# A hybrid layer on one core: a new written order for the recurrence's blocks, a low-rank product on full rows, and two more blocks that read PSUM

## The chip, the cores and the metric

The kernel runs on one core of a Trainium2 chip. The metric is the device time of one execution in microseconds (us); the median of three runs is given. A core has TensorE (PE, which multiplies and writes to the accumulator memory PSUM; PEld is its weight load), VectorE (DVE), ScalarE (ACT), GpSimd (POOL) and SyncE (SP), whose queue issues most of the transfers here. All of them share the on-chip memory SBUF. Each engine works through its own list of instructions in order, and waits for the others by semaphores.

## What is computed

One decoder layer on 2048 tokens of width 1024. Two mixers read the same normalised input, their outputs are joined by `w_out`, and a gated feed-forward part follows. All of it is float32 in the reference:

```python
xn = _rms_norm(h, pre_mix_norm[l])
proj = (xn @ w_in[l]).astype(jnp.float32)
p_ssd, p_rwkv = jnp.split(proj, [SSD_COLS], axis=-1)
y_ssd = _ssd_mixer(p_ssd, ...)        # causal conv of 4 taps, chunked scan, gate, norm
y_rwkv = _rwkv7_mixer(p_rwkv, ...)
mix = jnp.concatenate([y_ssd, y_rwkv], axis=-1).astype(h.dtype) @ w_out[l]
h = h + _rms_norm(mix, post_mix_norm[l])
```

The part that the change touches is the second mixer (8 heads of 64), together with the projections and the causal convolution of the first:

```python
p = p + (_token_shift(p) - p) * mu                       # this token mixed with the one before
r, w_lo, k, v, a_lo, g_lo = jnp.split(p, ...)
w_log = -softplus(-(w0 + tanh(w_lo) @ w2)) - 0.5         # two low-rank products, 64 rows each
a = sigmoid(a0 + a_lo @ a2)
kk = heads(k * k_k); kk = kk / max(norm(kk), 1e-12)
# per token: S = S * decay + (S @ -kk) (kk * a)^T + v k^T ;  y = S @ r
```

## The kernel before

`phase_R` computes the recurrence and the shared projections, `phase_S` the first mixer's scan and the output projection, and the feed-forward part comes last. The change touches `phase_R`, which works on 16 blocks of 128 tokens. In iteration `it` the block `it` is the front (`f`): its input is projected. The block before it (`b`) is finished behind it, the block two back (`a`) gets its last norm and store, and the next one (`n`) is loaded.

A block's work is cut into named steps (the methods of `Block`), and a step into numbered parts. For a front these are:

- `d.g` (14 of them) and `c`, written `conv.g` (8): float16 products of the block with a weight tile, 24 matmuls each at L324. Two neighbours share one PSUM bank of tag `mm`, which has two buffers. From `d`, ScalarE takes this token's part and VectorE adds the previous token's (`past`, L535). From `c`, ScalarE begins the sum of four taps in `ca` (L571) and VectorE adds six taps for the pair (L581); then come a tanh (L587) and a product (L592).
- `low.i`: the two low-rank products into `zw` and `za`. Weights and values are split into a high and a low half in float16. Four matmuls at L622 use all 128 rows, four at L626 the 64 rows of `wl`'s third plane.
- `scan`, `keys`, `norm`: running sums of the decay into `Pv`, their exponentials `Pi` and `Pv`, the keys' norm (product `nq` at L667, Ln L678, Exp L679, `kkn` L680), the scaled keys `tk` (L683), and the matrices `AR` (L684, L700) and `BK` (L688, L690).
- `gram.c`, for the two halves `c` of a block: products `gr` of `AR` with `BK` (L713), masked into `G` (L718).
- `solve`: the small triangular systems. `G`'s corners go to DRAM and back into `atl`; then 31 pairs of a product (L753) and a sum (L759) on VectorE run through them, and the result goes over DRAM (`XTd`, L765) back into `XT` (L771), in four transfers.

For the back block follow `turn` (transposes `XW`, L824), `merge` (products `pw` L840 and `po` L844), `own.c` (`pq`: the local products L873 and those with the state L879), `update.c` (`pu`, L897), `state.c` (`pS` L921, the new state `S` L927, the reads L932 into `pq`), `gate` (`zg`) and `finish` (norm, the transposes `yt`, the output `yo` and its store `YR`, L1000).

The order is written out by hand. `FIRST` holds for iteration 0, `SECOND` for 1, `PLAN` for 2 to 14, `LAST` for 15 and `DRAIN` for 16. An entry `f.norm/2` is part 2 of the front's step `norm`; where VectorE, ScalarE, GpSimd and SP run under `manual_schedule`, each engine gets its instructions in the order of the table. `PLAN` is one period of a loop that is wound around: the parts of a block's solve from some step on stand at the start of the table, for the block before. At iterations 2 and 15 the loop `if it in (2, iters - 1)` first emits those parts that the period before or after would have held.

A block whose `direct` is true lets ScalarE and VectorE read `d` and `c` from PSUM. Otherwise a copy is made first (`raw` in `d`, `rc` in `conv`), GpSimd begins the taps, and `scan` gets one more Ln of a single column (L651). Before, `direct` was true for the blocks 2 to 14.

Of the kernel before, what the change touches and what calls it, by code (L numbers as in the profile page):

```python
# [18 lines left out]
P = 128  # L19
# [198 lines left out]
PLAN = """  # L218
b.solve/30 b.solve/31 b.d.13/1 b.solve/32 b.solve/33 f.d.0 f.d.1/0 f.d.1/1 a.finish.0/1 b.conv.5/10 b.solve/34
a.gate/1 b.solve/35 b.d.13/3 b.d.13/4 n.load/1 b.solve/36 f.d.2 b.solve/37 b.solve/38 f.d.1/2 f.scan/2 a.finish.0/2  # L220
b.solve/39 a.state.1/3 a.finish.0/3 a.finish.0/4 f.d.1/3 b.values/0 b.solve/40 a.finish.1/0 b.solve/41 b.solve/42
b.solve/43 b.solve/44 b.solve/45 f.low.0/0 b.values/1 f.low.0/1 f.low.0/2 b.solve/46 b.solve/47 b.solve/48
a.finish.1/1 b.solve/49 b.solve/50 b.solve/51 b.values/3 b.values/4 f.d.1/4 b.transposed.1/1 a.finish.1/2 b.solve/52
a.finish.1/3 a.finish.1/4 b.conv.5/11 f.d.3/0 f.low.1/0 f.low.1/1 f.low.1/2 a.finish.1/5 b.values/2 b.own.0/0 f.d.3/1
f.d.3/3 b.solve/53 f.low.0/3 f.d.4 b.solve/54 b.solve/55 f.d.3/2 f.low.0/4 f.d.5/0 b.conv.7/9 a.finish.1/6 f.d.3/4
b.solve/56 b.conv.7/10 f.d.5/2 f.low.1/5 f.d.5/4 f.d.5/1 f.low.1/9 f.d.6 f.d.5/3 f.keys/0 b.solve/57 b.solve/58
f.d.7/0 a.finish.1/7 f.low.1/6 f.keys/1 f.low.1/3 b.solve/59 f.low.1/7 f.d.8 f.d.7/2 b.solve/60 b.solve/61 b.solve/62
b.solve/63 f.low.1/8 b.solve/64 f.norm/0 f.low.1/4 b.solve/65 f.d.7/1 b.solve/66 b.solve/67 f.norm/1 f.d.7/4 f.scan/0
a.state.1/4 f.norm/2 b.solve/68 b.solve/69 b.solve/70 f.d.7/3 b.own.0/1 b.solve/71 f.scan/1 a.finish.1/8 f.norm/4
f.norm/5 f.norm/7 b.solve/73 f.norm/6 b.solve/74 b.state.0/0 f.d.9/0 f.d.9/2 f.norm/3 f.scan/3 f.d.9/4 f.d.9/1 f.d.9/3  # L230
n.load/0 b.solve/72 f.norm/9 f.conv.0 b.solve/75 f.scan/4 f.norm/10 b.solve/76 f.conv.1/0 f.conv.1/1 f.conv.1/2
f.conv.2 f.conv.1/3 f.conv.1/5 f.conv.1/4 f.conv.1/6 b.conv.7/11 f.conv.3/0 f.conv.1/8 b.solve/78 f.conv.1/7
f.conv.3/1 f.conv.3/2 b.turn/0 f.norm/8 b.turn/1 f.conv.4 b.own.0/2 f.conv.1/9 f.load/10 b.merge.0/0 f.conv.3/3
f.conv.3/4 f.receptance/0 f.norm/11 a.finish.1/9 b.merge.0/2 f.conv.3/6 f.conv.5/0 f.norm/12 b.solve/77 b.merge.0/1
b.merge.1/0 f.gram.0/0 n.load/2 n.load/3 b.merge.1/2 b.merge.1/1 f.conv.1/10 b.update.0/0 f.conv.3/8 f.gram.1/0
f.conv.1/11 f.conv.3/5 f.conv.3/7 f.gram.0/1 f.conv.3/9 f.conv.3/10 f.gram.0/2 f.solve/8 b.update.0/1 n.load/4
f.solve/1 f.gram.1/2 f.gram.1/1 b.state.0/5 f.conv.5/1 f.conv.5/2 b.state.0/2 f.solve/0 n.load/5 f.conv.6 f.conv.5/3
n.load/6 f.transposed.0/0 b.state.0/3 f.conv.3/11 f.solve/2 f.conv.5/4 f.receptance/3 f.conv.5/5 b.state.0/1
f.conv.5/6 f.conv.7/0 b.state.0/6 b.own.1/0 b.state.0/4 f.receptance/2 f.conv.7/1 b.low.0/6 f.conv.7/3 f.solve/3
f.solve/4 f.solve/6 f.solve/5 f.conv.7/2 f.conv.7/4 f.receptance/1 f.conv.5/8 f.conv.7/5 b.state.1/0 f.conv.7/6  # L240
b.own.1/1 f.transposed.0/1 f.conv.7/8 b.state.1/1 f.solve/7 n.load/8 f.conv.5/7 f.transposed.1/0 f.conv.7/7 f.solve/9
b.gate/0 f.solve/10 b.own.1/2 b.update.1/0 f.d.10 f.conv.5/9 f.solve/11 n.load/7 f.d.11/0 f.receptance/4 f.solve/12
f.solve/13 f.solve/14 f.d.12 f.solve/15 f.solve/16 f.solve/17 f.solve/18 f.solve/19 f.solve/20 f.solve/21 f.solve/22
f.solve/23 f.solve/24 f.d.11/1 f.solve/25 f.solve/26 b.update.1/1 b.state.1/2 b.state.1/5 f.d.13/0 f.low.0/5 f.d.11/2
f.transposed.0/2 f.solve/27 f.d.11/4 b.state.1/6 b.finish.0/0 n.load/9 f.solve/28 f.solve/29 f.d.11/3 f.d.13/2
"""
# [82 lines left out]
def phase_R(tc, K, const, tables, x, w_r, w_c, wl_d, g2_d, XN, XC, YR, filler, iters=16):  # L329
    nc = tc.nc  # L330
    V, S, G_ = nc.vector, nc.scalar, nc.gpsimd
    with ExitStack() as ctx:
# [85 lines left out]
        class Block:  # L418


            def __init__(self, it):
                self.it, self.sf, self.direct = it, f"_{it}", 1 < it < iters - 1
                self.todo, self.m = {}, {}
# [86 lines left out]
            def d(self, g):  # L510
# [86 lines left out]
            def low(self, part):  # L597
# [19 lines left out]
                def products(i):  # L617
                    own, X = sides[i][0], self.X
                    ps = m["z", i] = self.ms(("zw", "za")[i])
# [4 lines left out]
                    for j in range(4):  # L624
                        js = slice(j * P, (j + 1) * P)
                        nc.tensor.matmul(  # L626
                            ps[:, j, :], wl[own, 2, js], X[own, i], start=False, stop=j == 3, skip_group_check=True)

# [389 lines left out]
        for it in range(iters + 1):  # L1018
# [10 lines left out]
            if it in (2, iters - 1):  # L1029
                for step in PLAN.split():  # L1030
# [1160 lines left out]
```

## Time and profile before

| | us |
|---|---|
| median of 3 runs | 2577.92 (2576.6 to 2578.97) |
| the profiled execution | 2581.0 |
| its span | 2579.2 |
| mean granted TensorE clock | 0.978 of full speed |
| `phase_R` until `d_0` of block 15 | 832.75 |
| 13 planned blocks, `d_0` to `d_0` | 688.16, from 144.59 to 832.75 |
| a planned block | 52.04 to 58.51 |
| block 15, to `phase_S`'s first products | 61.65 |

The starts of `d_0` of the blocks 0 to 15 lie at 15.06, 90.07, 144.59, 198.74, 250.79, 302.83, 355.34, 407.72, 460.30, 512.35, 564.45, 617.39, 675.90, 727.96, 780.00 and 832.75. The page's engine shares are averages over three phases with different limits. What the change does in `phase_R` has to be read from windows of its blocks: how long each takes, how much of that TensorE is busy, at what clock, and which wait ends last.

### The profile page before, as it was taken

The numbers are of one execution on the slowest core, as the hardware profiler recorded it, in microseconds if no ns is written. First come the engines' busy times: TensorE is split into PE (matmuls) and PEld (weight loads), VectorE is DVE, ScalarE is ACT, GpSimd is POOL, SyncE is SP. The second block draws the span as 40 slices with busy tenths as digits, with TensorE's granted clock in tenths as the row PEclk, the third lists the DMA queues.
The fourth block names the chain that finished last, engine by engine and source line by source line (L and its number), as shares of the span: only waits on it lengthen the run. The fifth ranks groups of instructions, "written<-read, shape, count | busy, mean of one in ns | idle before, by whom it ended". The sixth has DMA issues, their size and how long they took to land. (4 is left out here: it accounts for less than half of the span.)

```text
span 2579.2 us, 53771 instructions
## 1 busy us (share of the span) xinstructions
PE 2421.4 (94%) x21197; PEld 1528.3 (59%) x21212; DVE 1965.7 (76%) x3687; ACT 1209.7 (47%) x2415; POOL 1242.9 (48%) x1252
## 2 busy tenths in 40 slices
PE   5899999999999889999988999999989999999998
PEld 4789989998899755555433444444434444444443
DVE  7778888888788656768788789999999826455557
ACT  7555665566555544444544554544543432213132
POOL 2333444334343534446687675775858522223135
PEclk8999999999999989999998999999999999999999
DMA  7332233322332344555665444444436543333242
GB/s 220 75 65 65 55 74 73 72 55 63 68 78 67 127 144 128 144 160 170 165 212 169 162 143 174 142 172 172 140 131 210 161 135 103 102 102 102 86 159 107
DMA packets 344413, 319.13 MB, mean 124 GB/s; under 512 B 203232, under 2 KB 248672, under 8 KB 340832
## 3 DMA queue, kind: packets, MB, share of 16 engines
q1 hardware_dynamic: 342864, 314.12, 40.9%
q8 instruction: 166, 2.72, 0.4%
q10 hardware_dynamic: 1296, 1.58, 0.2%
q14 instruction: 87, 0.71, 0.1%
HBM read 187.85 MB, written 110.99 MB: 116 GB/s over the span
## 5 line engine op out<-in xcount | busy, mean ns | idle before, releaser
L1657 PE MATMUL u<-b,w 128*128 128x512 f16 x3696 | 811.2, 382 | 27.8 <-DVE C L1675 7.8
L1657 PEld LDWEIGHTS <-w 128*128 128x128 f16 x3696 | 363.2, 98 | 472.8 <-issue 36.9
L324 PE MATMUL d<-xt,wr 128*128 128x129 f16 x5376 | 336.2, 225 | 18.3 <-DMA xt<-xh 15.1
L324 PEld LDWEIGHTS <-wr 128*128 128x128 f16 x5376 | 322.0, 101 | 34.8 <-ACT wr L287 15.0
L1893 PE MATMUL d<-dw,fa 128*128 128x512 f16 x1512 | 333.6, 380 | 4.7 <-DMA dw<-DW 2.3
L1893 PEld LDWEIGHTS <-fa 128*128 128x128 f16 x1596 | 156.8, 98 | 205.7 <-issue 19.1
L1675 DVE TENSOR_TENSOR C<-u,C 128x512 f32<-128x512 f32 x220 | 150.5, 684 | 156.4 <-PE u L1657 151.2
L324 PE MATMUL c<-xt,wc 128*128 128x131 f16 x3072 | 196.4, 225 | 25.3 <-DVE ca L581 13.9
L324 PEld LDWEIGHTS <-wc 128*128 128x128 f16 x3072 | 184.1, 99 | 32.0 <-issue 25.0
L1906 DVE TENSOR_TENSOR acc<-d,acc 128x512 f32<-128x512 f32 x212 | 140.1, 682 | 54.3 <-PE d L1893 53.4
L1503 POOL TENSOR_TENSOR fa<-p,fa 128x512 f16<-128x512 f32 x100 | 142.2, 1435 | 40.1 <-ACT fa L1498 40.1
L1505 DVE SCALAR_TENSOR_TENSOR w<-us,w 128x512 f16<-128x512 f32 x132 | 145.8, 1115 | 14.9 <-ACT w L1498 13.7
L1710 DVE SCALAR_TENSOR_TENSOR p<-C,fpar,p 128x1024 f32<-128x1024 f32 x88 | 128.8, 1464 | 35.4 <-ACT p L1706 35.2
L1710 DVE SCALAR_TENSOR_TENSOR a<-C,fpar,a 128x1024 f32<-128x1024 f32 x88 | 125.7, 1429 | 4.4 <-ACT a L1706 3.0
L1498 ACT ACTIVATE fa<-p 128x512 f16<-128x512 f32 x110 | 65.5, 623 | 132.4 <-DVE p L1723 120.5
L759 DVE TENSOR_TENSOR xl<-xl,tmp 128x60 f32<-128x60 f32 (+24 forms) x465 | 117.7, 253 | 12.0
L1629 POOL TENSOR_TENSOR us<-us,us 128x512 f32<-128x512 f32 x66 | 106.0, 1609 | 41.9 <-DVE w L1505 22.4
L1671 ACT ACTIVATE C<-u 128x512 f32<-128x512 f32 x88 | 52.2, 593 | 145.8 <-PE u L1657 128.9
L1716 POOL COPY fcarry<-C 128x2 f32<-128x2 f32 x88 | 41.1, 468 | 163.4 <-DVE C L1675 163.4
L1498 ACT ACTIVATE w<-us 128x512 f16<-128x512 f32 x132 | 80.6, 624 | 78.8 <-POOL us L1629 45.4
L753 DVE TENSOR_TENSOR tmp<-atl,xl 128x60 f32<-128x60 f32 (+24 forms) x465 | 100.3, 216 | 20.8 <-DMA atl<-ATd 3.2
L581 DVE SCALAR_TENSOR_TENSOR ca<-c,cw,ca 128x128 f32<-128x128 f32 x312 | 96.8, 340 | 14.3 <-ACT ca L571 12.0
(323 smaller groups left out, 4518.1 us busy)
## 6 DMA issues: line engine op xcount, KB each, us to landing
UW<-w SPq DMA_DIRECT2D x154, 256.0 KB
w<-UW SPq DMA_DIRECT2D x154, 256.0 KB
us<-in_w_u_dram SPq DMA_DIRECT2D x88, 256.0 KB
DW<-dw SPq DMA_DIRECT2D x70, 256.0 KB
dw<-DW SPq DMA_DIRECT2D x56, 256.0 KB
hs<-HN SPq DMA_DIRECT2D x48, 256.0 KB
r<-in_w_d_dram SPq DMA_DIRECT2D x10, 1024.0 KB
xin<-in_x_dram SPq DMA_DIRECT2D x16, 512.0 KB
```

The source lines that it names most:

```text
L324: nc.tensor.matmul(ps, w[:, a, kt, :], xt[:, b, kt, cols], start=n == 0, stop=n == 3 * KT - 1)
L753: chain.tensor_tensor(out=self.tmp[:, :k, :n], in0=self.atl[:, j, j + 1:32].unsqueeze(1).to_broadcast([P, k, n]), in1=self.xl[:, :k, j:j + ...
L759: chain.tensor_tensor(out=self.xl[:, :k, j + 1:32], in0=self.xl[:, :k, j + 1:32], in1=self.tmp[:, :k, :n], op=ALU.add)
L1498: S.activation(h, src, AF.Copy, **({} if scale is None else {"scale": scale}))
L1503: {"V": V, "G": G_}[engine].tensor_tensor(out=l, in0=src, in1=h, op=ALU.subtract)
L1505: V.scalar_tensor_tensor(out=l, in0=src, scalar=scale, in1=h, op0=ALU.mult, op1=ALU.subtract)
L1629: op("G", 1.25, lambda: G_.tensor_tensor(out=st[o], in0=st[a], in1=st[b], op=alu), (n[a], n[b]), (n[o],))
L1657: nc.tensor.matmul(bk[at], self.w[i][:, u, k, :], self.half.b[i][:, k, v, :], start=start and n == 0, stop=n == 11, skip_group_check=True)
L1675: op("V", .61, lambda: V.tensor_tensor(out=part(j, x), in0=bk[at], in1=part(*a), op=ALU.add), (("u", 4 * s + at), (*(c0, c1)[a[0]], a[1])) ...
L1710: V.scalar_tensor_tensor(out=o[j], in0=C[j][:, 2 - d:1026 - d], scalar=cw[:, g, 2 - d:3 - d], in1=o[j], op0=ALU.mult, op1=ALU.add)
L1893: nc.tensor.matmul(bk[s, t], pairs[m].a[i][:, u, t * P:t * P + P], pairs[m].w[n][0][:, v, :], start=new and m == 0 and u == v == 0, stop=m ...
L1906: V.tensor_tensor(out=acc[j][:, t], in0=bk[s, t], in1=acc[j][:, t], op=ALU.add)
```

## The change

It has four parts.

1. **A new `PLAN`** for the iterations 2 to 14. The parts are the same; where a block begins in the table is different (at solve step 35 instead of 30), and so is the order inside. On TensorE the two `gram` products stand side by side, the state's products L879 come after `c_0`, the local products L873 of the first half directly behind `nq`, `pw` between `c_2` and `c_4`, and `zg`, `pS` and the reads behind the second half of `c_4`.
2. **The low-rank product on 128 rows.** `wl` gets a fourth plane; two planes are filled with zeros on GpSimd, the low half of each weight lies in its own plane, and the products of L626 (L627 after) run over all 128 rows.
3. **`direct` for all blocks but 0.** Blocks 1 and 15 lose the copies to SBUF and the Ln of one column, and ScalarE begins their taps. Block 0's copies lie in the buffers `yln` and `tg`.
4. **The steps emitted ahead of iteration 15** take the `a` entries of the late steps as well, so that `a.finish.0` of block 13 is emitted there.

```diff
-R_LEFT = ("sq", "kkn", "thw", "tha", "Pv", "xin", "wl", "wr", "tk", "BK", "ca cth", "raw", "xt", "wc")
+R_LEFT = ("sq", "kkn", "thw", "tha", "Pv", "xin", "wl", "wr", "tk", "BK", "ca cth", "xt", "wc")
...
 PLAN = """
-b.solve/30 b.solve/31 b.d.13/1 b.solve/32 b.solve/33 f.d.0 f.d.1/0 f.d.1/1 a.finish.0/1 b.conv.5/10 b.solve/34
...
+f.d.0 b.solve/35 a.state.1/6 b.solve/36 b.solve/37 a.finish.0/0 b.solve/38 f.d.1/0 b.d.13/2 b.conv.7/9 b.d.13/1
...
-        wl = wk.tile([P, 3, 512], F16, name="wl")
+        wl = wk.tile([P, 4, 512], F16, name="wl")
+        G_.memset(wl[:, 2:4], 0.0)
...
-                    out=wl[rows, 2], in0=st[rows], scalar=WS, in1=wl[rows, i], op0=ALU.mult, op1=ALU.subtract)
+                    out=wl[rows, 2 + i], in0=st[rows], scalar=WS, in1=wl[rows, i], op0=ALU.mult, op1=ALU.subtract)
...
-                self.it, self.sf, self.direct = it, f"_{it}", 1 < it < iters - 1
+                self.it, self.sf, self.direct = it, f"_{it}", it > 0
...
                 def raw():
-                    m["raw", e] = wk.tile([P, 2, 129], F32, name=f"raw{sf}_{e}", tag="raw", bufs=2)
-                    S.activation(m["raw", e], m["d", e][:, :, 0:129], AF.Copy)
+                    m["raw", e] = wk.tile([P, 2, 256], F32, name=f"raw{sf}_{e}", tag=("yln", "tg")[e // 2 % 2])
+                    S.activation(m["raw", e][:, :, 0:129], m["d", e][:, :, 0:129], AF.Copy)
...
-                own, X = sides[i][0], self.X
+                X = self.X
...
-                            ps[:, j, :], wl[own, 2, js], X[own, i], start=False, stop=j == 3, skip_group_check=True)
+                            ps[:, j, :], wl[:, 2 + i, js], X[:, i], start=False, stop=j == 3, skip_group_check=True)
...
-                    elif who == "b" and (name, *a) != ("finish", 1):
+                    elif who in "ab" and name in LATE and (name, *a) != ("finish", 1):
                         blocks[it - 2].do(name, *a)
```

What the table does to the engines is best seen in their lists. The names below carry the number that the program gives to each tile; `kkn`, `tk`, `AR`, `BK` and `ca_0` are of the front (block 7), `XW` and `XT` of the back. First VectorE before, from `kkn` to `BK`:

```order
L680 SCALAR_TENSOR_TENSOR kkn_7685<-sq_7716,kkn_7685 128x512
L535 SCALAR_TENSOR_TENSOR tr_7581<-d_8_7721,mus,tr_7581 128x128 x2
L475 COPY xt_7817<-xt_6787 128x16x3
L684 SCALAR_TENSOR_TENSOR AR_7820<-kkn_7685,Pi_7474 128x4x128
L581 SCALAR_TENSOR_TENSOR ca_0_7875<-c_0_7822,cw,ca_0_7875 128x128 x6
L824 STREAM_TRANSPOSE XW_7938<-XT_231 32x256
L683 TENSOR_TENSOR tk_7580<-tk_7580,tm_7778 128x512
L824 STREAM_TRANSPOSE XW_7938<-XT_231 32x256
L581 SCALAR_TENSOR_TENSOR ca_2_7935<-c_2_7878,cw,ca_2_7935 128x128 x2
L700 TENSOR_TENSOR AR_7820<-tr_7581,Pi_7474 128x4x2x64
L688 SCALAR_TENSOR_TENSOR BK_7992<-tha_7558,sq_7716 128x4x128
```

And the same place on VectorE with the new table:

```order
L681 SCALAR_TENSOR_TENSOR kkn_7655<-sq_7749,kkn_7655 128x512
L684 TENSOR_TENSOR tk_7564<-tk_7564,tm_7754 128x512
L582 SCALAR_TENSOR_TENSOR ca_0_7842<-c_0_7784,cw,ca_0_7842 128x128 x5
L825 STREAM_TRANSPOSE XW_7884<-XT_229 32x256 x2
L582 SCALAR_TENSOR_TENSOR ca_0_7842<-c_0_7784,cw,ca_0_7842 128x128
L689 SCALAR_TENSOR_TENSOR BK_7889<-tha_7627,sq_7749 128x4x128
L593 SCALAR_TENSOR_TENSOR ca_0_7842<-ct_0_7891,ca_0_7842 128x256
L685 SCALAR_TENSOR_TENSOR AR_7986<-kkn_7655,Pi_7464 128x4x128
L701 TENSOR_TENSOR AR_7986<-tr_7565,Pi_7464 128x4x2x64
L582 SCALAR_TENSOR_TENSOR ca_2_7983<-c_2_7859,cw,ca_2_7983 128x128
```

`AR` (L684, now L685) moved from ahead of the six taps of `c_0` to behind them and behind `BK`; `tk` moved ahead of them, and the transposes `XW` stand ahead of the sixth tap. On TensorE the product `pw` needs these transposes. Its neighbours in block 7 before, then with the new table:

```order
L324 LDWEIGHTS wc
L324 MATMUL c_4_7942<-xt_6787,wc 128x131
L840 MATMUL pw_7972<-XW_7938,G_7052 32x32 x16
L324 LDWEIGHTS wc
L324 MATMUL c_4_7942<-xt_6787,wc 128x131
```

Before, `pw` stood between the two halves of `c_4`.

```order
L324 LDWEIGHTS wc
L324 MATMUL c_2_7859<-xt_6480,wc 128x131
L841 MATMUL pw_7918<-XW_7884,G_7005 32x32 x16
L324 LDWEIGHTS wc
L324 MATMUL c_4_7941<-xt_6480,wc 128x131
```

It moved ahead of `c_4`, directly behind `c_2`. The third place is SP's queue around the return of the solve of the back block, before (`XC` is the store of `ca`, `XN` that of the block's turned input, `YR` that of the block two back):

```order
L765 DMA XTd_7773<-xl_7058 256x1x32 x4
L771 DMA XT_231<-XTd_7773 32x8x32 x2
L594 DMA XC_68<-ca_6_7170 128x2x128
L771 DMA XT_231<-XTd_7773 32x8x32
L507 DMA XN_60<-xt_6787 2048x1x128
L1000 DMA YR_75<-yo_7713 1024x1x128
L771 DMA XT_231<-XTd_7773 32x8x32
L594 DMA XC_68<-ca_0_7875 128x2x128
L742 DMA xl_8088<-in_cst_dram 128x256
```

And after:

```order
L766 DMA XTd_7747<-xl_6997 256x1x32 x4
L772 DMA XT_229<-XTd_7747 32x8x32 x2
L595 DMA XC_68<-ca_6_7164 128x2x128
L772 DMA XT_229<-XTd_7747 32x8x32
L1001 DMA YR_75<-yo_7572 1024x1x128
L772 DMA XT_229<-XTd_7747 32x8x32
L341 DMA xin_7989<-in_x_dram 128x1024
L743 DMA xl_8027<-in_cst_dram 128x256
```

The store of `XN` moved out from between the third and the fourth `XT`; the store of `YR` stays there.

More of the change, by code (lines that the diff above doesn't have):

```diff
@@ L218 @@
 PLAN = """
-b.solve/30 b.solve/31 b.d.13/1 b.solve/32 b.solve/33 f.d.0 f.d.1/0 f.d.1/1 a.finish.0/1 b.conv.5/10 b.solve/34
[L220 to L243, printed above, removed]
@@ L244 @@
-f.solve/23 f.solve/24 f.d.11/1 f.solve/25 f.solve/26 b.update.1/1 b.state.1/2 b.state.1/5 f.d.13/0 f.low.0/5 f.d.11/2
-f.transposed.0/2 f.solve/27 f.d.11/4 b.state.1/6 b.finish.0/0 n.load/9 f.solve/28 f.solve/29 f.d.11/3 f.d.13/2
+f.d.0 b.solve/35 a.state.1/6 b.solve/36 b.solve/37 a.finish.0/0 b.solve/38 f.d.1/0 b.d.13/2 b.conv.7/9 b.d.13/1
+a.finish.0/1 b.solve/39 b.solve/40 b.solve/41 b.solve/42 b.solve/43 b.solve/44 b.solve/45 b.solve/46 a.finish.0/2
+b.transposed.0/2 b.d.13/3 b.values/3 b.d.13/4 a.finish.0/3 f.d.1/1 f.d.1/2 f.d.2 b.conv.5/11 f.scan/2 b.solve/47
@@ new lines @@
+a.finish.0/4 f.d.1/3 a.finish.1/0 f.low.0/0 b.values/0 b.solve/48 f.low.0/1 f.d.1/4 f.low.0/3 b.solve/49 f.d.3/0
+n.load/0 b.transposed.1/1 b.solve/50 b.solve/51 f.low.0/2 f.low.0/4 a.finish.1/1 b.solve/52 a.finish.1/4 b.solve/53
+a.finish.1/2 b.solve/54 a.state.1/3 a.finish.1/3 a.finish.1/5 b.solve/55 b.solve/56 f.low.1/0 f.d.4 b.values/4 f.d.3/1
+f.d.3/2 f.d.3/4 f.d.3/3 a.finish.1/6 a.finish.1/7 f.load/10 f.d.5/0 f.d.6 b.solve/57 b.solve/58 f.low.1/1 f.low.1/3
+a.state.1/4 f.d.5/2 b.solve/59 b.solve/60 b.solve/61 b.solve/62 b.solve/63 b.solve/64 b.solve/65 f.low.1/5 f.d.5/1
@@ new lines @@
+b.values/1 f.d.5/3 f.d.5/4 f.low.1/4 f.low.1/6 f.keys/0 f.d.7/0 f.d.8 f.d.9/0 b.solve/66 f.low.1/2 f.scan/0 b.solve/67
+b.solve/68 f.low.1/9 b.values/2 f.d.7/2 b.conv.7/10 f.low.1/7 b.solve/69 b.solve/70 f.d.7/4 f.d.7/1 f.d.7/3 f.scan/1
+b.solve/73 f.keys/1 f.norm/0 f.low.1/8 f.norm/4 f.norm/5 f.norm/1 f.d.9/2 b.solve/72 f.d.9/1 b.own.0/0 f.norm/7
+b.solve/74 f.scan/3 f.norm/6 a.finish.1/8 b.solve/71 f.conv.0 f.norm/2 f.d.9/3 f.conv.1/0 b.solve/75 f.d.9/4 f.norm/3
+b.state.0/0 f.scan/4 f.norm/8 f.conv.1/1 f.conv.1/2 f.conv.1/4 b.own.0/1 f.conv.1/3 b.own.0/2 f.conv.1/6 f.norm/10
@@ new lines @@
+n.load/4 f.conv.5/0 b.gate/0 f.receptance/4 f.conv.3/9 f.conv.3/10 b.state.0/2 b.state.0/1 b.state.0/5 f.conv.5/1
+n.load/5 n.load/6 f.solve/1 b.state.0/4 f.solve/0 f.conv.5/3 f.conv.5/5 n.load/7 f.conv.5/2 f.solve/2 f.receptance/3
+f.conv.6 f.solve/3 f.conv.5/4 b.gate/1 f.conv.7/0 b.state.0/3 b.state.0/6 b.own.1/0 f.conv.5/6 b.own.1/1 b.state.1/0
+f.conv.3/11 f.conv.7/1 b.state.1/1 f.transposed.0/1 f.conv.5/8 f.conv.5/7 f.conv.7/2 f.conv.5/9 f.conv.7/3 f.conv.7/5
+f.conv.7/7 b.own.1/2 f.conv.7/4 f.solve/4 f.conv.7/6 f.conv.7/8 f.solve/5 f.conv.5/10 f.solve/6 f.d.10 f.d.11/0
```

13 lines of the change are left out of this document (11 added, 2 removed).

## The prediction

> **What bounds the kernel now.** I read the page's engine line first, then cut the program into blocks. A block begins where TensorE starts the first projection product `d_0` of a front (the timeline gives 407.72, 460.30, and so on). For each block I read the windows, then TensorE's waits, then the timeline around each wait.
>
> ```profile
> PE 2421.4 (94%) x21197; PEld 1528.3 (59%) x21212; DVE 1965.7 (76%) x3687; ACT 1209.7 (47%) x2415; POOL 1242.9 (48%) x1252
> ```
>
> TensorE is busy for 94% of the span, so time is lost only where it waits, runs at a lower clock, or changes its tile size. The change touches phase R alone, that is the first 894 us. The windows of four blocks (start and end, length, then busy time per engine with counts, granted clock, DMA share, GB/s):
>
> ```profile
> 90.07:144.59 54.52, 52.31 (x848) 48.78 (x846) 37.68 (x114) 30.13 (x69) 21.33 (x27) 0.97 0.29 68
> 407.72:460.30 52.58, 50.77 (x852) 47.33 (x850) 43.36 (x131) 31.35 (x70) 21.51 (x23) 1.00 0.29 67
> 617.39:675.90 58.51, 55.31 (x852) 51.55 (x849) 41.85 (x130) 31.46 (x70) 21.36 (x23) 0.91 0.28 61
> 832.75:894.40 61.65, 55.25 (x884) 50.93 (x882) 40.45 (x107) 31.95 (x77) 33.04 (x53) 0.94 0.38 132
> ```
>
> The rows are block 1, a usual planned block (7), block 11 and block 15. Block 7 takes 52.58 us, of which TensorE works 50.77: only 1.81 us are idle. VectorE works 43.36 of them, so it has slack in the mean but not everywhere. Block 11 lost 5.93 us against block 7, at a clock of 0.91. TensorE's waits over the 13 planned blocks (total us, times, longest), then over block 15:
>
> ```profile
> PE c L324 <- DVE ca L581: 13.9, 11, 1.3
> PE po L844 <- DMA XT<-XTd: 4.4, 6, 1.8
> PE c L324 <- ACT qs L885: 1.5, 1, 1.5
> PE c L324 <- ACT ca L571: 1.3, 1, 1.3
> ...
> PE nq L667 <- ACT sq L658: 3.5, 1, 3.5
> PE pw L840 <- DVE XW L824: 1.8, 2, 1.0
> ```
>
> One wait stands in every planned block: `c` waits 1.26 us for the taps of the pair before it (13.9 + 1.5 + 1.3 = 16.7 us in 13 blocks). The one behind it, `po` for the solve's return, comes in six blocks. Here is the place in block 7 on TensorE, then VectorE, GpSimd and ScalarE beside it (start, duration, instruction, idle before):
>
> ```profile
> 416.13 1.15 PE L873 MATMUL pq<-UV,G 64*64 64x64 f32 x32
> 419.98 0.39 PE L622 MATMUL za<-WX,wl 128*128 128x128 f16 x4
> 420.30 0.39 PE L626 MATMUL za<-WX,wl 64*128 64x128 f16 x4
> 420.62 4.31 PE L324 MATMUL d<-xt,wr 128*128 128x129 f16 x72
> 424.77 1.08 PE L667 MATMUL nq<-sq,cst 128*128 128x512 f32 x2
> 425.95 1.16 PE L879 MATMUL pq<-S,AR 128*128 128x128 f32 x8
> 428.32 5.76 PE L324 MATMUL c<-xt,wc 128*128 128x131 f16 x96
> 435.35 1.56 PE L324 MATMUL c<-xt,wc 128*128 128x131 f16 x24 [1.26 <-DVE ca L581]
> 436.84 0.69 PE L840 MATMUL pw<-XW,G 32*32 32x32 f32 x32
> ...
> 430.87 2.40 DVE L684 SCALAR_TENSOR_TENSOR AR<-kkn,Pi 128x512 f32<-128x512 f32 x1
> 433.19 2.02 DVE L581 SCALAR_TENSOR_TENSOR ca<-c,cw,ca 128x128 f32<-128x128 f32 x6
> 435.24 0.43 DVE L824 STREAM_TRANSPOSE XW<-XT 32x256 f32<-32x256 f32 x1
> 435.70 0.69 DVE L683 TENSOR_TENSOR tk<-tk,tm 128x512 f32<-128x512 f32 x1
> 438.22 0.68 DVE L688 SCALAR_TENSOR_TENSOR BK<-tha,sq 128x512 f32<-128x512 f32 x1
> ...
> 431.46 1.26 POOL L687 TENSOR_TENSOR sq<-kkn,Pv 128x512 f32<-128x512 f32 x1
> ...
> 426.37 0.69 ACT L678 ACTIVATE sq<-nq,tiny 128x512 f32<-128x512 f32 x1
> 427.07 1.28 ACT L679 ACT_TABLE_LOAD   x1
> 428.37 0.63 ACT L679 ACTIVATE sq<-sq 128x512 f32<-128x512 f32 x1
> 429.15 0.62 ACT L648 ACTIVATE Pi<-Pv 128x512 f32<-128x512 f32 x1
> ```
>
> The six taps end at 435.21 and `c_4`, which needs their PSUM bank, starts at 435.35. They began late because `AR` (L684) stood ahead of them and took 2.40 us, where an operation of the same size and kind (L688) takes 0.68. The excess of 1.72 us lies beside GpSimd's `sq` (L687) to 432.72; `AR` ends 0.55 us later.
>
> **The change part by part.** *The taps' wait.* In the new order `pw` stands between `c_2` and `c_4`, `AR` (L685) stands behind the first taps, and `tk` and five taps, the two transposes `XW` and then the sixth tap come straight behind `kkn`. What can be late now is `pw`, for `XW`. Count both sides from the end of `nq`. TensorE: the local products 1.15, `c_0` 2.88 (half of 5.76), the past products 1.16, `c_2` 2.88, together 8.1 us. The chain: the Ln 0.69, a table load 1.28, `Pi` 0.62, the Exp 0.63, `kkn` and `tk` 0.69 each, five taps 1.68 (five sixths of 2.02), two transposes 0.86, together 7.1 us, and six hand-overs between engines of some 0.1 to 0.2 (`c_4` started 0.14 after the taps' end) make 7.7 to 8.3. So it is nearly a tie. Then `gr` needs `AR` and `BK`: VectorE still has the sixth tap 0.34, `BK` 0.68, the tanh's product 0.41, `AR` 0.68 and its second half, 0.7 if undisturbed, in all 2.8; TensorE has `pw` 0.69, half of `c_4` 1.44 and `po` 0.69, also 2.8. A tie again. So the remaining wait is between 0 and 1.7 us a block (the latter if one of these operations is held as L684 was). I take 0.4, near the balance of the durations. Gain: 16.7 − 13 × 0.4 = 11.5 us.
>
> *The past products* now stand behind `c_0`. Before, `pq` started 1.18 us after `nq`, whose own work is 1.08; the price of the state's join there is at most 0.2 a block. The bounds are 0 and 2.6 us in 13 blocks; I take 1.5.
>
> *Tile sizes.* The four products of L622 and the four of L626 have equal columns; from 419.98 to 420.30 and 420.62 each four take 0.32 us. At the rate of the 72 behind them (4.15 us to 424.77, 57.6 ns each) four would take 0.23, so one change of tile size costs 0.09 us. The new order and the 128-row low-rank product take three changes out of each planned block (21 to 18): 39 × 0.09 = 3.5 us. The product on 128 rows itself adds nothing, since L622 on 128 rows shows the same 0.39 busy as L626 on 64. GpSimd's new zeroing of half of `wl` is a fill of 1024 two-byte values a partition at the start. It lies in front of work that waits anyway:
>
> ```profile
> 5.83 0.19 POOL L487 TENSOR_SCALAR pnv<-ss 128x1 f32<-128x1 f32 x1 [2.61 <-ACT xh L483]
> ```
>
> GpSimd is idle for 2.61 us there; the fill costs nothing while it is shorter than that, and I count 0.
>
> *The solve's return.* The solve's last step and SP's queue in block 7 (start, duration, transfer):
>
> ```profile
> 426.35 0.18 DVE L759 TENSOR_TENSOR xl<-xl,tmp 128x8 f32<-128x8 f32 x1
> ...
> 426.55 2.57 SPq L765 DMA_DIRECT2D XTd<-xl  x4
> 432.50 0.55 SPq L507 DMA_DIRECT2D XN<-xt  x1
> 433.15 1.14 SPq L1000 DMA_DIRECT2D YR<-yo  x1
> 434.34 1.27 SPq L771 DMA_DIRECT2D XT<-XTd  x1
> ...
> 650.55 0.69 PE L844 MATMUL po<-XT,XW 32*32 32x32 f32 x32 [1.85 <-DMA XT<-XTd]
> ```
>
> The solve's last step ends at 426.53 (18.8 us after `d_0` of 407.72), the fourth `XT` leaves 7.8 us later behind the stores of `XN` and `YR`, and its landing made `po` wait 0.45 at 439.50. In the new order eight more of the solve's steps (L753 and L759, about 0.2 each by the row) stand ahead of `d_0`'s first operation on VectorE, and the two `tr` of `d_6` and `d_7`, ahead of the last steps before, stand behind them now; so the solve no longer follows TensorE up to `d_7`. Counting through VectorE's order with the durations of this trace I estimate its end at 15.2 instead of 18.8. `XN` (0.55) is gone from between. That brings the landing forward by 4.1 to 4.9. `po` comes earlier as well: the wait of 1.26, half a `d` and half a `c` (1.44 each) no longer precede it, the local products (1.15) do, and with the 0.4 above it stands some 3.4 us earlier. Against a wait of 0.45 that leaves a margin of 0.2 to 1.0 us. It holds by little; I take all 4.4 us as gained, the bounds are 0 and 4.4. With it goes block 11's halving of the clock. It was granted 0.50 right behind the 1.85 us wait:
>
> ```profile
> 652.13:662.37 10.24, 10.24 (x98) 9.47 (x97) 5.96 (x14) 4.43 (x7) 3.54 (x4) 0.50 0.28 66
> ```
>
> Block 11's cost beyond the wait is 58.51 − 52.58, less the 1.40 by which its `po` wait is longer than block 7's 0.45, or 4.5 us. [...]
>
> *Block 15* now reads the projections from PSUM: ScalarE drops the copies and the Ln of one column with its table load:
>
> ```profile
> 847.29 1.28 ACT L651 ACT_TABLE_LOAD   x1
> 849.56 1.57 PE L667 MATMUL nq<-sq,cst 128*128 128x512 f32 x2 [3.47 <-ACT sq L658]
> ```
>
> `sq` of L658 followed that load and the 0.20 us Ln, so 1.5 of the 3.47 us go at once; with fewer copies I take 2.2, and 0.8 of the 1.8 for `pw`. Bounds: 0 and, with the low clock (0.94 over 61.65 us, about 3.7), 9.
>
> *Block 1* loses its copies too, but its taps now read PSUM and hold the bank, as in a planned block, where this costs 1.26 at one place. I take +1.0; bounds −1 and +3.
>
> **Sum.** −11.5 − 1.5 − 3.5 − 4.4 − 4.5 − 3.0 + 1.0 = −27.4 us. The profiled execution's span was 2579.2 and its time 2581.0; the median of the timed runs is 2577.9, 3.1 lower. So a span of 2551.8, a profiled 2553.6 and a timed 2550.5: **2550 us**.
>
> **Rivals.** *One: the wait moves and stays whole.* [...] Price: 1.7 instead of 0.4 a block, 13 × 1.3 = 16.9 us: 2567. [...]
>
> *Two: nothing but the tile changes.* If the waits only change their names, with the halved clock still somewhere, the gain is the 3.5 us of tile changes: 2574, which counts as no change.
>
> *Three, slower: the last `XT` waits for `YR`.* `YR` needs `yo`, GpSimd's last work of a block, and a queue issues in order. If `yo` comes late, `XT` and then `po` are late in every block. From 1.85 us a block on, the clock falls as at 650.55: 13 × (1.85 + 4.5) = 83 us in place of the 8.9 gained with `po` and block 11, and 2550 + 83 + 9 gives about 2640. It decides from the point where `yo` comes over 1 us later than the third `XT`, the margin above. For: the margin is small. Against: `yo` is written by GpSimd, busy 21.51 of 52.58 us in block 7, and the final store left within 1.2 us before.
>
> **How the numbers follow.** The forecast has 0.60, with a range of its own of 2543 to 2558 (waits of 0 to 1 us a block). Rival one has 0.25, rival two 0.06, rival three 0.06; 0.03 remains for a new wait on a PSUM bank that costs 10 to 25 us. The range's low end, 2541, is the forecast without the 0.4 us (−5.2) and with block 15 some 4 us better; its high end, 2571, is rival one with the 4.5 us of the clock kept. A measurement of this kernel tells 0.2%, about 5.2 us, from no change: faster below 2572.8 is 0.87, the same 0.06, slower 0.07.
>
> **What would show it.** In the profile of the changed kernel a planned block should take about 50.9 us, the list of waits should have no `c` behind taps above 0.3, `pw` and `gr` together under 0.5 us a block, no `po` behind `XT`, and no planned window with a clock below 1.00. L685 should show about 0.7 us; block 15 should take about 58 us with `nq` waiting about 1.3. Planned blocks at 52 with `pw` or `gr` behind VectorE would be rival one. `po` behind `XT` with `YR` just ahead on SP's queue would be rival three.

## The result, and the profile after

| | median us | runs | lowest to highest |
|---|---|---|---|
| before | 2577.85 | 4 | 2576.6 to 2578.97 |
| changed kernel | 2553.51 | 4 | 2552.7 to 2558.7 |

The ratio is 0.9910 with a 95% interval of 0.9893 to 0.9927: 24 us less, where 2550 was forecast. The profiled execution's span fell from 2579.2 to 2551.1, where the sum of the prediction gave 2551.8. The page's engine line, then the windows of block 1, of block 7, of block 11 and of block 15 (columns as before):

```profile
PE 2406.4 (94%) x21212; PEld 1520.3 (60%) x21212; DVE 1921.5 (75%) x3687; ACT 1204.6 (47%) x2407; POOL 1231.3 (48%) x1237
...
92.03:147.81 55.78, 51.76 (x848) 48.37 (x846) 36.04 (x111) 30.03 (x66) 14.93 (x18) 0.97 0.25 57
402.86:453.15 50.29, 50.29 (x851) 47.35 (x849) 39.85 (x131) 31.14 (x70) 21.26 (x23) 1.00 0.35 70
604.00:654.29 50.29, 50.29 (x851) 47.35 (x849) 39.85 (x131) 31.14 (x70) 21.25 (x23) 1.00 0.34 71
807.22:864.51 57.29, 52.24 (x881) 48.57 (x882) 38.21 (x105) 29.86 (x70) 31.76 (x53) 1.00 0.42 142
```

The share of TensorE in the span is 94% as before: the page's first line says nothing about what happened. The windows do. A planned block takes 50.29 us and TensorE is busy in all of them; block 11 is like the others, at full clock. TensorE's waits over the 13 planned blocks, then over block 15:

```profile
PE d L324 <- DVE tmp L754: 2.6, 2, 1.3
PE yt L983 <- POOL ysb L975: 0.7, 1, 0.7
...
PE d L324 <- DVE tr L536: 1.4, 1, 1.4
PE pw L841 <- DVE XW L825: 1.1, 2, 0.9
PE nq L668 <- ACT sq L659: 1.0, 1, 1.0
```

In the planned blocks no `c` waits for taps and no `po` for the solve. What is left in the planned stretch lies in its first block; a wait of 1.91 us follows at its very end, ahead of `d_0` of block 15, and makes the last planned block 52.4 us. The view names no releaser for it; VectorE reads earlier products from PSUM (L536) until 807.12, 0.1 us ahead of it, but whether that holds it was not tested. Where the time went, from the starts of `d_0` in the two profiles:

| stretch | before | after | difference |
|---|---|---|---|
| until `d_0` of block 0 | 15.06 | 15.64 | +0.58 |
| block 0 | 75.01 | 76.39 | +1.38 |
| block 1 | 54.52 | 55.77 | +1.25 |
| 13 planned blocks | 688.17 | 659.41 | −28.76 |
| block 15 | 61.62 | 57.29 | −4.33 |
| `phase_S`, to the feed-forward's first product | 406.42 | 408.45 | +2.03 |
| feed-forward | 1278.43 | 1278.16 | −0.27 |

This is the place of the old wait in block 7's front, in the changed kernel: TensorE, then VectorE, GpSimd and SP's queue in the timeline (the back is block 6).

```profile
419.86 1.13 PE L668 MATMUL nq<-sq,cst 128*128 128x512 f32 x2
420.92 1.15 PE L874 MATMUL pq<-UV,G 64*64 64x64 f32 x32
422.00 2.97 PE L324 MATMUL c<-xt,wc 128*128 128x131 f16 x48
424.81 1.11 PE L880 MATMUL pq<-S,AR 128*128 128x128 f32 x8
425.75 2.96 PE L324 MATMUL c<-xt,wc 128*128 128x131 f16 x48
428.65 0.83 PE L841 MATMUL pw<-XW,G 32*32 32x32 f32 x32
429.42 1.57 PE L324 MATMUL c<-xt,wc 128*128 128x131 f16 x24
430.92 0.69 PE L845 MATMUL po<-XT,XW 32*32 32x32 f32 x32
431.54 2.08 PE L714 MATMUL gr<-AR,BK 64*128 64x128 f32 x32
...
425.08 0.69 DVE L681 SCALAR_TENSOR_TENSOR kkn<-sq,kkn 128x512 f32<-128x512 f32 x1 [1.85 <-ACT sq L680]
425.69 0.69 DVE L684 TENSOR_TENSOR tk<-tk,tm 128x512 f32<-128x512 f32 x1
426.30 1.51 DVE L582 SCALAR_TENSOR_TENSOR ca<-c,cw,ca 128x128 f32<-128x128 f32 x5
427.84 0.90 DVE L825 STREAM_TRANSPOSE XW<-XT 32x256 f32<-32x256 f32 x2
429.84 0.67 DVE L685 SCALAR_TENSOR_TENSOR AR<-kkn,Pi 128x512 f32<-128x512 f32 x1
...
425.94 1.56 POOL L688 TENSOR_TENSOR sq<-kkn,Pv 128x512 f32<-128x512 f32 x1 [1.60 <-PE pq L880]
427.48 1.26 POOL L691 TENSOR_TENSOR BK<-tk,Pv 128x512 f32<-128x512 f32 x1
...
418.66 2.56 SPq L766 DMA_DIRECT2D XTd<-xl  x4
425.27 0.56 SPq L1001 DMA_DIRECT2D YR<-yo  x1
425.87 0.66 SPq L772 DMA_DIRECT2D XT<-XTd  x1
```

Three things are to be seen. `AR` (L685) takes 0.67 instead of 2.40: GpSimd's `sq` and `BK` have ended at 428.74, before it starts. While they run, VectorE has taps and transposes, and these take their usual 0.3 and 0.45 each; `tk`, which started 0.25 us ahead of `sq`, takes its usual 0.69, and `sq` 1.56 instead of 1.26. The transposes end at 428.74 and `pw` starts at 428.65, nearly the tie that was counted out: no idle time is put down to it, but its products stretch over 0.77 us to the next start where they need 0.63 (a run below shows this), so 0.14 of a wait hides inside. And the solve's last step ended at 418.63, 15.8 us after `d_0` (the row of its first store, 418.66, follows at once), where 15.2 was estimated.

### The profile page after: what moved, and what is told of

The parts are those of the page before. It is cut to its first block, busy times and chain, and to the rows that moved or that the text cites. A ratio compares the mean times of both kernels' runs of the same rounds, so it can differ in the third digit from the quotient of the medians.

```text
span 2551.1 us, 53834 instructions
## 1 busy us (share of the span) xinstructions
PE 2406.4 (94%) x21212; PEld 1520.3 (60%) x21212; DVE 1921.5 (75%) x3687; ACT 1204.6 (47%) x2407; POOL 1231.3 (48%) x1237
## 5 line engine op out<-in xcount | busy, mean ns | idle before, releaser
L324 PE MATMUL d<-xt,wr 128*128 128x129 f16 x5376 | 333.1, 224 | 25.1 <-DMA xt<-xh 15.6
L1907 DVE TENSOR_TENSOR acc<-d,acc 128x512 f32<-128x512 f32 x212 | 140.2, 683 | 52.7 <-PE d L1894 51.8
L582 DVE SCALAR_TENSOR_TENSOR ca<-c,cw,ca 128x128 f32<-128x128 f32 x360 | 113.5, 344 | 25.3 <-ACT ca L572 21.4
L754 DVE TENSOR_TENSOR tmp<-atl,xl 128x60 f32<-128x60 f32 (+24 forms) x465 | 119.1, 256 | 17.4 <-DMA atl<-ATd 5.9
```

Source lines behind the costliest of these rows:

```text
L324: nc.tensor.matmul(ps, w[:, a, kt, :], xt[:, b, kt, cols], start=n == 0, stop=n == 3 * KT - 1)
L582: V.scalar_tensor_tensor(out=acc[:, q], in0=m["rc", e][:, q, k:k + 128], scalar=cw[:, e + q, k:k + 1], in1=acc[:, q], op0=ALU.mult, op1=AL ...
L754: chain.tensor_tensor(out=self.tmp[:, :k, :n], in0=self.atl[:, j, j + 1:32].unsqueeze(1).to_broadcast([P, k, n]), in1=self.xl[:, :k, j:j + ...
L1907: V.tensor_tensor(out=acc[j][:, t], in0=bk[s, t], in1=acc[j][:, t], op=ALU.add)
```

## The experiments

Five questions were open: which of the parts does it; whether `AR` was held by GpSimd; whether `po` hung on the order in SP's queue; what a change of tile size costs in place; and whether the waits that appear in blocks 0 to 2 and behind block 15 can be mended. Medians are compared with runs of the kernel before on the same chip, since its median differs between the chips, from 2576.57 to 2582.53 us.

**The new table alone.** The kernel before with the new `PLAN` and the steps ahead of iteration 15 that go with it:

```diff
-b.solve/30 b.solve/31 b.d.13/1 b.solve/32 ...
+f.d.0 b.solve/35 a.state.1/6 b.solve/36 ...
...
-                    elif who == "b" and (name, *a) != ("finish", 1):
+                    elif who in "ab" and name in LATE and (name, *a) != ("finish", 1):
```

> The kernel before with the new table for blocks 2 to 14 (and the steps emitted ahead of iteration 15 that belong to it), low-rank product on 64 rows and blocks 1 and 15 with their copies as before. Theory (the order alone removes the taps' wait, the po waits and block 11's halved clock): the 13 planned blocks take 659.4 us as in the changed kernel plus four tile-size changes of 0.09 each a block, 4.7 us, so about 664 instead of 688; no c and no po wait; block 15 stays near 61.6; time 2552 to 2557. Rival (the full rows or the PSUM reads of the neighbours are needed for it): planned blocks stay above 675 us, time above 2565.

Measured: 2553.69 us (2552.0 to 2555.0, 4 runs) against 2582.53 on that chip, ratio 0.9897 (0.9873 to 0.9922). A planned block of its profile:

```profile
400.90:451.40 50.50, 50.50 (x849) 47.20 (x848) 39.81 (x131) 31.09 (x71) 21.23 (x24) 1.00 0.31 70
```

The planned blocks take 659.8 us in all, and there is no `c` and no `po` wait: the theory holds, the rival falls. Its own first planned block takes 51.36 us instead of 53.90. So the new order by itself carries the gain.

**One entry of the old table moved.** `AR` directly behind `kkn`, so that it does not meet GpSimd's products:

```diff
-f.norm/3 f.scan/3 f.d.9/4 f.d.9/1 f.d.9/3 n.load/0 b.solve/72 f.norm/9
+f.norm/3 f.scan/3 f.norm/9 f.d.9/4 f.d.9/1 f.d.9/3 n.load/0 b.solve/72
```

> The kernel before with one entry of the old table moved: the first half of AR (L684) directly behind kkn on VectorE, ahead of two operations on tr, so that it ends before GpSimd starts its product for sq. Theory (AR was held for 1.7 us by GpSimd's products, and this made the taps late): L684 takes about 0.7 instead of 2.4 us, the c wait of 1.26 falls below 0.3 in every planned block; po then comes 1.1 us earlier but the solve's return does not, so po waits 0.5 to 1.5 us in most blocks and eats most of the gain: 2568 to 2577, with a halved clock in blocks where the po wait nears 1.8. Rival one (AR is long by itself): L684 stays at 2.4, c waits as before, no change. Rival two (the solve's return has slack): no more po waits than before, 13 x 1.1 = 14 us, 2563.

Measured: 2590.77 us (2581.7 to 2608.1, 10 runs) against 2582.53, ratio 1.0040 (1.0016 to 1.0064): slower. The view of L684 (duration in ns: least, median, most), the waits of TensorE over the planned blocks, and the timeline at one `po`:

```profile
L684 DVE SCALAR_TENSOR_TENSOR AR<-kkn,Pi x10: 746/747/750, 273.3 to 750.0; 128x512 f32<-128x512 f32 x10
...
PE po L844 <- DMA XT<-XTd: 10.5, 11, 2.1
PE c L324 <- DVE tr L535: 6.6, 13, 1.8
...
336.35 0.78 PE L844 MATMUL po<-XT,XW 32*32 32x32 f32 x32 [2.12 <-DMA XT<-XTd]
337.06 2.08 PE L713 MATMUL gr<-AR,BK 64*128 64x128 f32 x16
```

`AR` takes 0.75 us in the ten blocks of the view and in the other three; in the kernel before it took 2.40 in all 13. So it was held beside GpSimd's products, and rival one falls. The wait for the taps is gone too. But `c` now waits 0.5 us for the `tr` that stand behind `AR`, and `po`, which comes earlier, waits in 11 of 13 blocks, 10.5 us instead of 4.4. Two of these waits, 2.12 and 1.98, are followed by a halved clock: 16 products `gr` take 2.08 us instead of 1.16, and the two blocks 59.7 and 58.0. The mechanism came as expected; the total was expected at 2568 to 2577 and was above the kernel before. In the profiled execution two planned blocks had the halved clock, where the profile before has one, and all 13 took 692.3 us instead of 688.2.

**Two entries moved.** In addition the fourth return of the solve directly behind the third, ahead of the stores of `XN` and `YR`:

```diff
-b.conv.7/11 f.conv.3/0 f.conv.1/8 b.solve/78
+b.conv.7/11 f.conv.3/0 f.conv.1/8 b.solve/78 b.solve/77
```

> The kernel before with two entries of the old table moved: AR behind kkn as in old_order_AR_first, and the fourth return of the solve (b.solve/77) directly behind the third on SP's queue, ahead of the stores of XN and YR. Theory (po waited because the last return stood behind two stores): the po waits of 10.5 us in 13 blocks fall below 2, no halved clock in the planned blocks, these take 668 to 675 us instead of 692; 2562 to 2570. Rival (the return is late because the solve ends late, and its place in the queue costs less than the transfer's own 5 us): po waits stay above 5 us, planned blocks above 678.

Measured: 2565.81 us (2562.1 to 2572.3, 6 runs) against 2581.15, ratio 0.9945 (0.9921 to 0.9968). TensorE's waits over the planned blocks:

```profile
PE c L324 <- DVE tr L535: 5.6, 13, 0.8
PE yt L982 <- POOL ysb L974: 2.1, 1, 2.1
PE pu L897 <- ACT XT L853: 0.3, 2, 0.2
PE po L844 <- ACT XW L851: 0.2, 1, 0.2
```

No `po` waits for the return any more; the planned blocks take 672.6 us, and only the first has a stretch of halved clock (3.4 us at 153, behind a `yt` wait of 2.1). So the place in SP's queue was the cause, and the rival falls. Two entries give 15 of the 29 us that the whole table gives. Of the rest 5.6 us is the `c` wait for `tr`, and the first planned block takes 55.4 us instead of the table's 51.4.

**PSUM reads in blocks 1 and 15 alone.** `direct` for all blocks but 0, and block 0's copies in `yln` and `tg`:

```diff
-                self.it, self.sf, self.direct = it, f"_{it}", 1 < it < iters - 1
+                self.it, self.sf, self.direct = it, f"_{it}", it > 0
```

> The kernel before with only direct for blocks 1 and 15 (block 0's copies in the buffers yln and tg). Theory: block 15 falls from 61.6 to about 57.3 us, block 1 grows from 54.5 to about 55.8, planned blocks stay at 688; time 2573 to 2576. If the 2.0 us by which the next phase grew in the changed kernel come with block 15's PSUM reads (ScalarE's casts of wo queued ahead of sz), they appear here too: the wait of z for sz near 7 us. Rival (that wait comes from the new table): no wait of z above 1 us here.

Measured: 2579.96 us (10 runs) against 2582.53, ratio 0.9996 (0.9977 to 1.0015): no difference, though the interval leaves room for the 3 us that were expected. Block 15 takes 58.6 us instead of 61.6, block 1 54.7. The planned blocks, whose order is the old one, take 682.4 us in this profile and not 688, since no halved clock falls into them and `po` waits less. TensorE's longest wait in the 43 us behind block 15, of this kernel, then of the changed kernel:

```profile
PE z L1215 <- ACT sz L1221: 8.0, 1, 8.0
...
PE z L1216 <- ACT sz L1222: 7.7, 1, 7.7
```

With the new table alone there is no such wait of `z`; there `bc` waits 1.9 us. So the wait of `z` comes with the PSUM reads. What it costs in all isn't shown: `phase_S` took 409.1 us here and 406.4 before, but 407.2 and 412.2 in two profiles of the new table alone, which lack this wait, and 406.5 to 408.5 in three of the changed kernel, which have it.

**The low-rank product on 128 rows alone.** The edit to `wl` and its products as in the diff, with the copies in `yln` and `tg`, for room. As `direct` is the old one here, these are the copies of blocks 1 and 15 too, and not of block 0 alone as the expectation has it:

> The kernel before with only the low-rank product on 128 rows (and block 0's copies in yln and tg, for room). Theory: four tile-size changes of 0.09 us less in a block, all of it ahead of nq; in the old order the taps wait behind nq moves along with TensorE and the solve's return does not, so 2 to 5.8 us less in 16 blocks, c waits unchanged at 1.26 or a little above; 2572 to 2576. The zeroing of wl costs 0.6 us at the start if the later start of block 0 in the changed kernel (15.64 instead of 15.06) came from it. Rival (64 and 128 rows cost the same, tile-size changes are free): no change in the planned blocks.

Measured: 2587.17 us (10 runs) against 2582.53, ratio 1.0020 (0.9999 to 1.0040): no gain, perhaps a loss. The planned blocks take 683.8 us with no halved clock; `c` still waits 1.26 in each, and `pq` 0.3 for the state's join, now that TensorE arrives earlier. So the time saved ahead of these waits became a wait itself. Beside this, `nq` waits 7.2 us in block 15 and a product of the next phase 9.6. The first of these goes, by the trace, with the place of the copies and not with the 128 rows: ScalarE's third copy of `d`, on whose values `nq` rests, started 9.8 us after `d_0` in the kernel before and starts 17.0 us after it here, where it waits for GpSimd's use of `yln`:

```profile
844.86 0.39 ACT L530 ACTIVATE raw<-d 128x258 f32<-128x258 f32 x1 [0.85 <-POOL yln L997]
```

So this run doesn't measure the 128 rows alone; the comparison with L626's 64 rows below does. The start is no measure of the zeroing of `wl`: `d_0` of block 0 came between 14.7 and 15.6 us in all profiles, with and without it.

**Three trials on the end of block 15 and on block 1.** In the changed kernel ScalarE's first two casts of `wo` stand ahead of the `sz` that frees `z`'s bank, and wait for a transfer that leaves behind the last solve's return:

```profile
887.20 2.42 ACT L287 ACTIVATE wo<-ost,sng 128x1024 f16<-128x1024 f32 x2 [7.96 <-DMA ost<-in_w_o_dram]
...
883.27 0.44 DVE L825 STREAM_TRANSPOSE XW<-XT 32x256 f32<-32x256 f32 x1 [6.99 <-DMA XT<-XTd]
```

The changed kernel itself, on the same chip as the trials:

> The changed kernel itself, as the measure for the three beside it on the same chip. 2551 to 2556 us; planned blocks 659.4, block 1 near 55.8, first planned block near 53.9, block 15 near 57.3, z waits about 7.7 us for sz.

Measured: 2549.02 us (2545.4 to 2550.2, 4 runs) against 2576.57, ratio 0.9895 (0.9880 to 0.9910), a little less than expected: block 1 took 54.2, the first planned block 52.8, block 15 56.3, and `z` waited 7.7. First the casts behind the gate of the second chunk:

```diff
+            pace(tc, K, d, "gated")
...
+                if self.n == 1:
+                    K.marks["gated"] = d
```

> The changed kernel, with ScalarE's casts of wo (which wait for a transfer issued behind the last solve's return) kept behind the gate (th) of the second chunk. Theory (ScalarE's queue held the gate's sz behind the casts, and z waited 7.7 us for it): the z wait falls below 1 us; part of it returns at bc, which waited 2.2 us in the kernel before; 3 to 6 us less than the changed kernel. Rival (the stretch is bound by block 15's solve, which ends at the same time): the wait moves to bc or pw in full, no gain above 1 us.

Measured: 2549.82 us (2548.3 to 2552.9), no gain. TensorE's first wait there is now

```profile
PE bc L1265 <- DVE dv L1165: 6.5, 1, 6.5
```

The wait moved to `bc`, nearly whole. On VectorE the casts' other half and the transposes `XW`, which wait for the last solve (a chain on GpSimd in block 15), stand ahead of what `bc` needs. The rival holds: freeing one queue is not enough.

Then `direct` for blocks 2 to 15 only (`it > 1`):

> The changed kernel with direct for blocks 2 to 15 only: block 1 makes its copies again (in the buffers yln and tg). Theory (block 1's taps hold the PSUM banks that block 2's first products want): block 1 falls from 55.8 to about 54.5, the first planned block from 53.9 to about 51.4 us, so 3 to 4 us less than the changed kernel. Rival (the buffers yln and tg, which block 0's norm and gate use in the same iteration, now make block 1's copies wait): block 1 above 56, no gain.

Measured: 2556.62 us (2549.0 to 2559.0), no gain. Block 1 fell to 52.8, but the first planned block took 53.3, as it does with the new table where block 1 reads PSUM (52.7 to 53.9), and `phase_S` took 415.4 instead of 408.0, with the clock halved for 17 us from 907 on. Where the border between the two blocks falls varies, so they are better taken together. Block 1 and the first planned block take 107.1 to 109.7 us in the five profiles of the new table with `direct` from block 1 on, and 105.5 to 106.1 in the four with block 1's copies (this run, the next, and the table alone twice). So block 1's PSUM reads cost about 1 us or more under the new table, where the prediction had 1.0; the totals do not show it.

> Both of the edits just named on the changed kernel. If they are independent, their gains add: 6 to 10 us less than the changed kernel, 2544 to 2548.

Measured: 2552.15 us (2550.1 to 2555.5): the gains that were to add up were not there. None of the trials beats the changed kernel.

**What the other two parts add to the table.** Three kernels on one chip, against 2579.11 before:

> The changed kernel, as the measure for the two beside it on the same chip: planned blocks 50.25 to 50.30 us each, 2548 to 2554.

> The new table alone on the kernel before, again. Theory (the low-rank product on full rows and the PSUM reads of blocks 1 and 15 cancel with what they cost around blocks 0 to 2 and at the end of block 15): planned blocks 50.5, block 15 near 60, and a time within 3 us of the changed kernel. Rival (they are worth their 0.22 us a planned block and the 3 us of block 15): 5 to 7 us more than the changed kernel.

> The changed kernel with the low-rank product's second half on 64 rows again (L626's form). Theory: TensorE is the bound in the planned blocks and has four tile-size changes more: 50.5 instead of 50.3 us a block, 2.9 us in 13; by the 0.09 us per change that the prediction used it would be 0.36 a block and 4.7. 1 to 5 us more than the changed kernel. Rival (the full rows cost as much as they save): no difference in the planned blocks.

Measured, six runs each: the changed kernel 2553.58 (2548.6 to 2558.7), the table alone 2554.56 (2552.8 to 2556.7), the changed kernel with L626's 64 rows 2558.24 (2556.2 to 2562.0). The planned blocks take 50.27, 50.51 and 50.51 us. So the 128 rows are worth 0.24 us a block, 2.8 us in all, and the last of the three is slower, as the theory said, though the spreads touch. The table alone lies within the spread of the changed kernel: whether the two other parts leave a gain of a us or so can't be told from these runs. Their place on TensorE, with 64 rows and then with 128:

```profile
413.06 0.39 PE L622 MATMUL za<-WX,wl 128*128 128x128 f16 x4
413.38 0.40 PE L626 MATMUL za<-WX,wl 64*128 64x128 f16 x4
413.70 4.31 PE L324 MATMUL d<-xt,wr 128*128 128x129 f16 x72
```

```profile
412.15 0.39 PE L623 MATMUL za<-WX,wl 128*128 128x128 f16 x4
412.38 0.39 PE L627 MATMUL za<-WX,wl 128*128 128x128 f16 x4
412.60 4.30 PE L324 MATMUL d<-xt,wr 128*128 128x129 f16 x72
```

The eight products take 0.64 us with two changes of tile size around L626 and 0.45 without: 0.095 each, as predicted. Two such pairs should save 0.38 a block, and 0.24 come out. The missing 0.14 is in `pw`: with 64 rows its products take 0.63 to the next start, with 128 rows 0.77, since TensorE now arrives a little ahead of the transposes: with 64 rows these end some 0.27 ahead of `pw`'s first product, with 128 rows 0.09 behind it. This is the wait that no list shows.

## Why the prediction was right, step by step

That the span came out at 2551.1 where the sum gave 2551.8 is partly luck. The parts that the sum named gained 4.4 us more than forecast; those that it set at nothing (the start, block 0, `phase_S` and the feed-forward part) took 3.7 back.

- **The taps' wait** (−11.5 forecast). The wait of 16.7 us is gone, and its cause, `AR` held beside GpSimd, is shown by moving `AR` alone. The balance of `pw` was called a tie with a remaining wait of 0.4 us a block, and measured 0.14.
- **Tile sizes** (−3.5) and **past products** (−1.5). 0.095 us a change is shown; the past products were tested by no run of their own. From start to start, TensorE's steps in block 8, which has no wait of `po` before, give the whole way from 52.05 to 50.29: `c` −1.40 (of which the wait is 1.26), the low-rank products −0.39, `gr` −0.17, `nq` −0.12, `pw` +0.15, and all others +0.17. The taps, the tile sizes and the past products were to give 1.27 us in such a block and gave 1.76. In the sum of the planned blocks (−28.8, forecast −25.4) this is partly hidden, since the first and the last of them, 53.9 and 52.4 us, have waits that the sum had not.
- **The solve's return** (−4.4) and **the clock** (−4.5). No planned block of the changed kernel has such a wait or a halved clock, and two moved entries show that `po` hung on the queue's order. The margin was as thin as forecast, and not by the forecast's count: in block 7 the solve ended at 15.8 and not 15.2 us, the last `XT` left 3.6 us earlier than before and not 4.1 to 4.9, and `po` came 3.7 earlier. By this count some wait would have stayed. None did: the time from `XT` to `po` is not fixed. It was 2.6 to 5.6 us where `po` waited, in the two kernels with the old place in the queue, and 4.6 to 5.8 with no wait in the changed kernel's blocks from 229 us on. The clock's term belongs to the execution that was profiled: the old table's planned blocks took 682.4 and 683.8 us, with no halved clock, in the profiles of direct_alone and low_alone. Three `po` waits, of 1.85 us in the kernel before and of 1.98 and 2.12 us in old_order_AR_first, were each followed by a halved clock within 2 us, and the changed kernel, with no wait of that length between 148 and 805 us, was granted 1.00 there. The high end of the range kept these 4.5 us; no planned block of the changed kernel has them.
- **Block 15** (−3.0, measured −4.33). `nq` waits 0.98 instead of 3.47, and the halved clock is gone as well in this profile (in after_five one stretch of 3.4 us came back), which the bounds had but the sum had not. What the sum left out is the next phase: the PSUM reads bring a `z` wait of 8 us there, by themselves too. That phase grew by 2.0 in the profile, but by 0.1 and 1.6 in the two other profiles of the same kernel.
- **Block 1** (+1.0, measured +1.25 in this profile, −0.3 and −0.1 in the two other profiles of the same kernel). By itself its sign is not settled; together with the first planned block a price of about 1 us or more is seen, as said above.
- **The zeroing of `wl`** at 0 is not contradicted: the start varies by 0.9 us among the seven profiles that have it, and lies between their ends in the seven that have not. Block 0 took 74.4 to 76.8 in three profiles of the changed kernel, so its +1.38 can't be told from this spread either.
- **Rival one** did not come: what VectorE runs beside GpSimd's `sq` and `BK` now is taps and transposes, and these were not stretched. `AR` took 2.40 beside GpSimd and 0.67 or 0.75 away from it, the transposes 0.45 beside `BK`. `tk` met `sq` for 0.4 us and kept its 0.69; there it was `sq` that grew, from 1.26 to 1.56. **Rival three** did not come either. old_order_AR_first shows what late returns cost, in kind and not in size: 11 `po` waits and two halvings made a slower kernel out of a better place for `AR`, but most of these waits stayed under 1.2 us, and the kernel was 8 us slower and not 83.

## What to carry to other kernels

When a wait is removed, ask at once what is due next on the same engine and how much slack it has: here some 0.8 us a block taken from one wait went to a transfer behind two stores in a queue, and with the halved clock behind two of the new waits it cost more than it gave. In a loop that runs at one engine's pace, balance both sides of each hand-over from the trace's durations; the tie at `pw` came out within 0.3 us. And where part of the order is left to a scheduler, compare its lists as well: reading PSUM in block 15 brought a wait of 8 us in the next phase. Before a part is tried alone, ask what else its edit moves: the low-rank product brought the copies of blocks 1 and 15 into other buffers, and a wait of 7 us came with them.

## What was not expected of the hardware

Rival three took the clock to fall from a wait of 1.85 us on, as it did at 650.55. TensorE's waits over 1.5 us between 120 and 900 us in the profiles of the kernel before and of the changed kernel, and the granted clock:

| profile | wait, us | until | granted clock |
|---|---|---|---|
| before | 1.89, `pq` in block 1 | 131.97 | 0.50 from 133.31 to 136.72 |
| before | 1.54, `c` in the first planned block | 174.32 | 1.00 until 652.13 |
| before | 1.85, `po` in block 11 | 650.55 | 0.50 from 652.13 to 662.37 |
| before | 3.47, `nq` in block 15 | 849.56 | 0.50 from 850.11 to 853.52 |
| before | 2.34, `pq` behind block 15 | 899.92 | 0.50 from 901.31 to 904.72 |
| after | 1.76, `c` in block 1 | 131.49 | 1.00 until 887.40 |
| after | 1.91, `d_0` of block 15 | 807.22 | 1.00 until 887.40 |
| after | 7.70, `z` in `phase_S` | 890.16 | 0.50 from 887.40 to 894.23 |

In these two profiles the length of one wait alone does not decide it: behind 1.91 us in the changed kernel the clock stayed at 1.00, behind 1.85 and 1.89 in the kernel before it fell to 0.50. And in block 15 before it was 0.50 from 860.35 to 863.76 behind two waits of 0.97 and 0.82 at `pw`. What else decides it was not shown. One kernel's executions can differ in it: block 15 of the changed kernel has no halved clock in the profile above, and a stretch of 3.4 us in after_five.

The three halved stretches of 10 us and more in planned blocks made these 6 to 8 us longer than their neighbours: block 11 before, and the two blocks of 59.7 and 58.0 us in old_order_AR_first. This may be why the kernels with `po` waits vary more: 25 runs of the kernel before on one chip lay between 2569.5 and 2593.1, 10 of old_order_AR_first between 2581.7 and 2608.1, and the new table alone, on two chips, between 2552.0 and 2556.7 in 10. No run tested this by itself.
